# Bank reads of VectorE at the front of its queue, forget gate and keys on ScalarE, later norm sums, and another priority for h rows in a hybrid decoder layer

## The chip, the cores and the metric

The kernel runs on one core of a Trainium2 chip. The metric is the device time of one execution in microseconds (us), as the median of several runs. The engines are TensorE (PE, with its weight loads shown apart as PEld), VectorE (DVE), ScalarE (ACT), GpSimd (POOL) and SyncE (SP), which issues most of the transfers. Each has its own queue of instructions; semaphores tie them together.

## The reference

One decoder layer over 2048 tokens of width 1024, in float32. A token mixer (RMSNorm with scale and shift from a conditioning vector, one combined input projection, three groups of heads, a gated norm per head, an output projection) is followed by a channel mixer (a second norm, an up-projection, a causal convolution of width 3, a SiLU-gated product, a down-projection) and a last norm. The change touches the token mixer. For one group of heads, HGRN2, it computes:

```python
z = split_heads(hf, HG_HEADS)
lbh = lb.reshape(HG_HEADS, HG_DK)[None, :, None, :]
log_f = jnp.logaddexp(jnp.log1p(-lbh) + jax.nn.log_sigmoid(z), jnp.log(lbh))   # f = lb + (1 - lb) * sigmoid(z)
key_h = (1.0 - lbh) * jax.nn.sigmoid(-z)
o_h = gated_state_chunkwise(jax.nn.silu(split_heads(hq, HG_HEADS)), key_h, split_heads(hi, HG_HEADS), log_f)
o_h = merge_heads(rms_norm(o_h)) * jax.nn.silu(hg)
```

`gated_state_chunkwise` is a linear recurrence whose state decays by `f` for each key channel: S_t = diag(f_t) S_(t-1) + k_t^T v_t, o_t = q_t S_t. The GLA heads use the same recurrence with another gate, the retention heads one with a fixed decay. The gate of each head's output is silu(g) = g * sigmoid(g).

## The kernel before

**Blocks and units.** The token mixer goes through the sequence in four blocks of 512 tokens (`b` is 0 to 3). In each block seven units follow one another (`ORDER`): HGRN2 units h0 and h1, the GLA unit g, h2, h3, and the retention units r0 and r1. A unit projects the block's normed rows `h` with its columns of the input weights and then starts a recurrence. After the units comes the first half of the output projection (`out_half(b, 0)`). The second half (`out_finish`) runs inside the next block's unit h1. The channel mixer (from about 1250 us on) is not changed.

**Matmuls.** Each float32 operand is split into a high and a low part, and each product takes three matmuls (`split3`, L254 to L256: high by high, high by low, low by high). The casts to the high part are on ACT, the subtractions for the low part on DVE. Projections write to four PSUM banks in turn (`acc_ps`). A bank is free for a later projection once all that read it are through. Two banks serve the levels of the recurrences (`lev_ps`), two the rest (`late_ps`: norm sums and spreads, state updates, outputs, transposes).

**A unit h** (`unit_h`) projects the forget gate into one bank. ACT takes sigmoid(z) (`sf`, L742) and sigmoid(-z) (`sn`, L743) from it. DVE makes f = sf * (1 - lb) + lb (L744) and the keys kq = sn * (1 - lb) (L745). The query projection goes into the next bank: ACT takes its sigmoid (L748), DVE multiplies the bank by it (L749). Then DVE's `near` (L611 to L615) and `decays` (L626) prepare the recurrence from queries, keys and f. Values and gates of a pair of units are projected together by `tf512` into four banks, one for every 128 tokens; `tok_evac4` takes them out: a copy of the values (ACT, L559), a sigmoid of the gate (ACT, L560), and the product of the gate with its sigmoid (DVE, L561), for each bank and each of two units. `tok_evac` (L550 to L552) does this for the first two units of the first block, which project alone.

**A recurrence** (`gated`) is a chain of short steps: two transposes and their sums for neighbouring tokens (L639, L643, L649), six levels of pairwise scores, each with matmuls (`lvh` or `lvg`, L662), then DVE's multiplication of queries and keys by the level's decay (L670, L672) and a masked copy (L681 on DVE, L678 on ACT). The matmuls of a level read the queries and keys that the level before has left. Then come the keys' transpose, the states' updates (`u` at L701; L709 and L711 on DVE), the outputs (L594, L596), the norm and gate of each head (`post`, L565 to L574), and later the transpose for the output projection (L580, L583, L584). `retention` is shorter.

**Order of the work.** PE's queue is in the order in which the program issues its matmuls. A small clock written by hand (`Clock`) sets that order: every piece of projection advances it by its estimated time, and `clock.at(us, fn)` has `fn` issued when the clock has come that much further. `clock.chain(gen, us)` puts a recurrence in line: it starts `us` later at the earliest, one chain at a time, and each step names the gap until the next. `clock.until(...)` issues what is due next, whatever the clock says, until a condition holds; `out_finish` inside unit h1 is preceded by such a call, for the last transposes of the block before (L1154).

The queues of DVE, ACT and SP are filled by a planner that works at build time: it simulates the engines, and of the instructions that it thinks ready it takes the one with the smallest number, which is its place in the program. `tc.high_priority(offset=n)` lowers the numbers inside by n. `HOT` is 600, `CHAIN` 400; the recurrences' DVE and ACT work runs at `CHAIN`, the low parts of the weights (L247, L316) and the additions to the residual (L986) at `HOT`. On the chip each queue runs in the order that the planner fixed.

**Norm of the next block.** `norm1_stat(b + 1)` squares and sums the next block's rows, as small jobs between projections. After the last, `clock.at(14.0, rstd(..., gap=9.5))` puts the sum over features (`ssn`, four transposes, L337, into a `late_ps` bank) 14 us later on the clock, and 9.5 us after that the spread of the reciprocal root over the partitions (`bcn`, L348). `norm1_h(b + 1)` then loads the rows again and makes `h`: `scaled` (DVE, L365), `high` (ACT, L369), `low` (DVE, L372), one row tile after the other, while the output projection and the last chains of block b run.

Of the kernel before, what the change touches and what calls it, by code (L numbers as in the profile page):

```python
# [14 lines left out]
AF = mybir.ActivationFunctionType  # L15
ALU = mybir.AluOpType
PSUM = bass.MemoryType.PSUM

P = 128
# [30 lines left out]
HOT = 600  # L50
CHAIN = 400
# [53 lines left out]
def trunk(ctx, tc, xT, vecs, cvec, cst, rope, msk, wada, win, walow, wgla, wout, wup, wdown, out):  # L105
# [13 lines left out]
    clock = Clock()  # L119
# [13 lines left out]
    def tmp(name, shape=(P, 512)):  # L133
        return pt.tile(list(shape), F32, tag="te", name=name, bufs=NTE)
# [4 lines left out]
    def small(name, n=8):  # L139
        return pc.tile([P, n], F32, tag="sm", name=name, bufs=8)  # L140

    V, S, G, T = nc.vector, nc.scalar, nc.gpsimd, nc.tensor
# [10 lines left out]
    def newton(x, y, n):  # L153

        V.tensor_scalar(y[:].bitcast(I32), x[:].bitcast(I32), -0.5, MAGIC, op0=ALU.mult, op1=ALU.add)
        a = small("nw", n)
        for _ in range(3):
            V.scalar_tensor_tensor(a[:], y[:], -0.5, y[:], op0=ALU.mult, op1=ALU.mult)
            V.tensor_tensor(a[:], a[:], x[:], op=ALU.mult)
            V.scalar_tensor_tensor(y[:], a[:], 1.5, y[:], op0=ALU.add, op1=ALU.mult)  # L160


    oml = p1.tile([P, 4], F32, tag="oml", name="oml")
    lb = p1.tile([P, 4], F32, tag="lb", name="lb")
# [99 lines left out]
    def cf_gemm(name, i, parts=(slice(0, TB),)):  # L264
        if name in ready:
            return ready.pop(name)
        hi, lo = piece(win[i], name, f"i{i}")
        ps = acc_ps("ps" + name)
        for ts in parts:
            for k in range(KD):  # L270
                sl = slice(k * P, (k + 1) * P)
                split3(ps[:, ts], (hi[:, sl], lo[:, sl]), (h[k][:, 0, ts], h[k][:, 1, ts]), k == 0, k == KD - 1)
                adv(3 * M512)
        return ps
# [55 lines left out]
    def rstd(acc, name, bc, then, bank=None, gap=4.5):  # L330

        bank = bank or late_ps

        def first():
            p = bank("ss" + name)
            for c in range(NCH):
                T.transpose(p[:, c * P:(c + 1) * P], acc[:, c * P:(c + 1) * P], ident)  # L337
            x, r = small("ms" + name, NCH), small("rs" + name, NCH)
            with tc.high_priority(offset=CHAIN):
                V.tensor_reduce(x[:], p[:].rearrange("p (c d) -> p c d", c=NCH), axis=mybir.AxisListType.X, op=ALU.add)  # L340
                V.tensor_scalar(x[:], x[:], 1.0 / D, EPS, op0=ALU.mult, op1=ALU.add)
                newton(x, r, NCH)
            clock.at(gap, lambda: second(r))

        def second(r):
            p = bank("bc" + name)
            for c in range(NCH):
                T.transpose(p[:, c * P:(c + 1) * P], r[:, c:c + 1].to_broadcast([P, P]), ident)  # L348
            S.copy(bc, p[:])
            then()  # L350
        return first

    def sumsq(acc, x, k, name, sl=slice(0, TB), first=None):
        if k == 0 if first is None else first:
            S.activation(acc[:, sl], x[:, sl], AF.Square)
        else:
            sq = late(f"sq{name}{k}")
            S.activation(sq[:, sl], x[:, sl], AF.Square)
            V.tensor_tensor(acc[:, sl], acc[:, sl], sq[:, sl], op=ALU.add)

    def new_acc(name):
        return px.tile([P, TB], F32, tag="ssacc", name="sa" + name, bufs=1)

    def scaled(t, bc, k):
        V.scalar_tensor_tensor(t, t, SC1[:, k:k + 1], bc, op0=ALU.mult, op1=ALU.mult)  # L365

    def high(t, k, name):
        h[k] = ph.tile([P, 2, TB], F32R, tag="h", name=f"ha{name}{k}", bufs=8)
        S.activation(h[k][:, 0, :], t, AF.Identity, bias=SH1[:, k:k + 1])  # L369

    def low(t, k):
        V.scalar_tensor_tensor(h[k][:, 1, :], t, SH1[:, k:k + 1], h[k][:, 0, :], op0=ALU.add, op1=ALU.subtract)  # L372

    xs = {}
    bc1 = {}
    done = set()
# [9 lines left out]
    def new_bc1(b):  # L386
        return px.tile([P, TB], F32, tag="bc1", name=f"bc1_{b}", bufs=1)
# [111 lines left out]
    def norm1_stat(b):  # L499
        acc = []  # L500

        def load(k):
            if not acc:
                acc.append(new_acc(f"n1_{b}"))
            x = tmp(f"x{b}_{k}")
            nc.sync.dma_start(x[:], xT[b, :, k, :])
            return x

        def add(x, k):
            sumsq(acc[0], x, k, f"n1_{b}_")  # L510
            if k == KD - 1:
                bc1[b] = new_bc1(b)
                clock.at(14.0, rstd(acc[0], f"n1_{b}", bc1[b][:], lambda: done.add(("n1", b)), gap=9.5))
        for k in range(KD):
            jobs.append((0.7, lambda k=k: load(k), lambda x, k=k: add(x, k)))

    def norm1_h(b):
        clock.until(lambda: ("n1", b) in done)
        for k in range(KD):
            t = tmp(f"xn{b}_{k}")  # L520
            nc.sync.dma_start(t[:], xT[b, :, k, :])
            scaled(t[:], bc1[b][:], k)
            high(t[:], k, f"{b}_")
            low(t[:], k)


    def new_qbd(name, rows):

        q = p1.tile([P, 2, TB], F32, tag="qbd", name="qb" + name, bufs=3)
        for hh in range(2):  # L530
            G.memset(q[64 * hh:64 * hh + 64, 1 - hh, :], 0.0)
            if rows[hh][1] - rows[hh][0] < 64:
                G.memset(q[64 * hh:64 * hh + 64, hh, :], 0.0)
        return q
# [5 lines left out]
    def tok_tiles(name):  # L540

        return (pu.tile([P, NCH, P], F32, tag="v", name="v" + name, bufs=4),
                pu.tile([P, NCH, P], F32, tag="sg", name="sg" + name, bufs=4))

    def tok_evac(vsg, pss):
        v, sg = vsg
        for j, ps in enumerate(pss):
            p3 = ps[:].rearrange("p (c n) -> p c n", n=256)
            c2 = slice(2 * j, 2 * j + 2)
            S.copy(v[:, c2, :], p3[:, :, 0:P])  # L550
            S.activation(sg[:, c2, :], p3[:, :, P:256], AF.Sigmoid)
            V.tensor_tensor(sg[:, c2, :], sg[:, c2, :], p3[:, :, P:256], op=ALU.mult)  # L552

    def tok_evac4(vsg, pss, at):

        v, sg = vsg
        for c, ps in enumerate(pss):
            gate = ps[:, at + P:at + 256]
            S.copy(v[:, c, :], ps[:, at:at + P])  # L559
            S.activation(sg[:, c, :], gate, AF.Sigmoid)  # L560
            V.tensor_tensor(sg[:, c, :], sg[:, c, :], gate, op=ALU.mult)  # L561

    def post(o, sg, name):

# [170 lines left out]
    def unit_h(b, u, pos, between=None):  # L735
        nm = f"h{b}_{u}"
        kq = pu.tile([P, TB], F32, tag="k", name="k" + nm, bufs=3)
        f = pu.tile([P, TB], F32, tag="f", name="f" + nm, bufs=3)
        e = pu.tile([P, TB], F32, tag="e", name="e" + nm)
        ps = cf_gemm("hf" + nm, 4 * u + 1)  # L740
        sf, sn = tmp("sf" + nm), tmp("sn" + nm)
        S.activation(sf[:], ps[:], AF.Sigmoid)  # L742
        S.activation(sn[:], ps[:], AF.Sigmoid, scale=-1.0)  # L743
        V.tensor_scalar(f[:], sf[:], oml[:, u:u + 1], lb[:, u:u + 1], op0=ALU.mult, op1=ALU.add)  # L744
        V.tensor_scalar(kq[:], sn[:], oml[:, u:u + 1], None, op0=ALU.mult)  # L745
        ps = cf_gemm("hq" + nm, 4 * u)
        sq = tmp("sq" + nm)
        S.activation(sq[:], ps[:], AF.Sigmoid)  # L748
        V.tensor_tensor(sq[:], ps[:], sq[:], op=ALU.mult)  # L749
        xy = near(sq, kq, f, nm)  # L750
        rows = [(0, 64), (64, 128)]
        q = new_qbd(nm, rows)
        for hh, (r0, r1) in enumerate(rows):
            V.tensor_tensor(q[r0:r1, hh, :], sq[r0:r1, :], f[r0:r1, :], op=ALU.mult)
        decay = decays(f, e)
        subs = [(q, rows, *tok_tiles(nm))]
        clock.chain(gated(nm, b, u, pos, kq, decay, subs, xy), 9.0 if b == u == 0 else 6.0)
        if b == 0 and u < 2:
            tok_evac(subs[0][2:], tf_gemm("vg" + nm, 4 * u + 2))
            tokens.add(nm)  # L760
            return
        waiting[nm] = subs[0][2:]
        if between:
            between()
        if u % 2:
            pss = tf512("vg" + nm, 4 * u - 2, 4)
            for i, one in enumerate((f"h{b}_{u - 1}", nm)):
                tok_evac4(waiting.pop(one), pss, 256 * i)
                tokens.add(one)
# [364 lines left out]
    for b in range(NB):  # L1134
        pos = 0
# [511 lines left out]
```

## Time and profile before

| | us |
|---|---|
| median of 3 runs | 2535.63 |
| lowest and highest run | 2533.63, 2539.6 |
| the profiled execution | 2533.2 |
| its span on the core | 2531.4 |
| token mixer, all blocks | about 60 to 1250 |
| channel mixer | about 1250 to 2531 |

The profile shows one execution, taken on the core by the hardware. Times are microseconds from the start of the span. A line with an engine, a kernel line and a tile name stands for a group of instructions; "<-" in a name leads from what is written to what is read. A row of waits names who waited for whom, the time in total, the number of waits and the longest. A row of stretches gives, after the stretch and its length, the busy time and number of instructions of PE, PEld, DVE, ACT and POOL, then PE's granted clock as a share of full speed, the share of the transfer engines, and GB/s. In a row of the timeline stand start, duration, engine, line, operation, tiles, and in brackets the idle time before it with what ended it. In a row of groups stand, after the count, the busy time, the mean in ns, and the idle time of the engine just before, with what ended it.

### The profile page before, as it was taken

To read this page: it belongs to the slowest core of one execution; us is meant where nothing else is said; L and a number is where in the kernel's file an instruction comes from. 1 tells how busy PE (TensorE), PEld (TensorE's weight loads), DVE (VectorE), ACT (ScalarE), POOL (GpSimd) and SP (SyncE) were. 2 spreads that over 40 slices of the span, in tenths; PEclk is the share of its full clock that TensorE was granted. 3 is DMA by queue.
4 is the path that set the end of the run, shared out by engine and by line. 5 is a ranking of instruction groups with operands and counts; after the bars stand their busy time and mean duration, and the time that the engine had idled before them with its cause. 6 is when DMAs were issued, how large, how long until landed. Compare 5 with 4: busy or idle time off the path is not lost.

```text
span 2531.4 us, 35178 instructions
## 1 busy us (share of the span) xinstructions
PE 2452.0 (97%) x12165; PEld 2059.3 (81%) x12165; DVE 1989.5 (79%) x3652; ACT 1147.5 (45%) x1950; POOL 146.3 (6%) x278
## 2 busy tenths in 40 slices
PE   5999999999999999999999999999989999999998
PEld 4888877888888888788788888888868888888887
DVE  8987887877688685877798888887678777778666
ACT  3334434434443434434554454455445545545442
POOL 1000000000000000000100000000001010010000
PEclk9999999999999999999999999999999999999999
DMA  8844458865689647884654544587665544447663
GB/s 312 296 159 134 169 169 322 290 234 169 215 283 318 224 157 241 311 300 158 222 190 147 171 147 141 168 283 243 209 199 186 159 137 152 150 133 263 213 196 126
DMA packets 232498, 525.11 MB, mean 207 GB/s; under 512 B 24928, under 2 KB 28032, under 8 KB 232320
## 3 DMA queue, kind: packets, MB, share of 16 engines
q1 hardware_dynamic: 229120, 512.38, 60.0%
q0 software_dynamic: 3200, 10.49, 1.2%
q8 instruction: 96, 1.57, 0.2%
q14 instruction: 82, 0.67, 0.1%
HBM read 397.46 MB, written 125.30 MB: 207 GB/s over the span
## 4 chain that ended last, share of the span: by engine, by line
PE 82%; DVE 8%; DMA 5%; issue 2%; ACT 1%; SPq 0%; DVEq 0%; POOL 0%; ACTq 0%; POOLq 0%
PE X L254 6%; PE X L256 6%; PE X L255 6%; PE Z L256 3%; PE Z L255 3%; PE Z L254 3%; PE lvh L662 3%; PE dX L256 3%; PE dX L255 3%; PE dX L254 3%; PE psqkvgr L254 2%; PE psqkvgr L256 2%; PE psqkvgr L255 2%; PE y L254 2%; PE y L256 2%
## 5 line engine op out<-in xcount | busy, mean ns | idle before, releaser
L254 PE MATMUL X<-B,A 128*128 128x512 f32 x572 | 224.4, 392 | 1.4 <-ACT u L1354 1.4
L255 PE MATMUL X<-B,A 128*128 128x512 f32 x572 | 223.9, 391 | 0.0
L256 PE MATMUL X<-B,A 128*128 128x512 f32 x572 | 223.6, 391 | 0.0
L1055 DVE TENSOR_TENSOR dA<-rd,dA 128x512 fp32r<-128x512 f32 x154 | 106.0, 689 | 87.6 <-ACT dA L1054 87.5
L1054 ACT CAST dA<-rd 128x512 fp32r<-128x512 f32 x154 | 95.6, 621 | 138.8 <-PE dY L256 42.2
L1055 DVE TENSOR_TENSOR A<-s,A 128x512 fp32r<-128x512 f32 x176 | 120.7, 686 | 40.7 <-ACT A L1054 40.3
L1054 ACT CAST A<-s 128x512 fp32r<-128x512 f32 x176 | 108.6, 618 | 68.0 <-PE Z L256 45.2
L254 PE MATMUL dX<-dB,dA 128*128 128x512 f32 x352 | 136.9, 389 | 0.0
L255 PE MATMUL dX<-dB,dA 128*128 128x512 f32 x352 | 136.9, 389 | 0.0
L256 PE MATMUL dX<-dB,dA 128*128 128x512 f32 x352 | 136.9, 389 | 0.0
L254 PEld LDWEIGHTS X<-B,A 128*128 128x128 f32 x572 | 108.2, 189 | 24.5 <-ACT u L1354 2.2
L255 PEld LDWEIGHTS X<-B,A 128*128 128x128 f32 x572 | 108.2, 189 | 22.7
L256 PEld LDWEIGHTS X<-B,A 128*128 128x128 f32 x572 | 108.2, 189 | 22.7
L255 PE MATMUL Z<-B,A 128*128 128x512 f32 x308 | 120.0, 390 | 2.2 <-DVE B L1055 2.2
L254 PE MATMUL Z<-B,A 128*128 128x512 f32 x308 | 119.9, 389 | 0.0
L256 PE MATMUL Z<-B,A 128*128 128x512 f32 x308 | 119.8, 389 | 0.0
L662 PEld LDWEIGHTS lvh<-qbh,kh 128*128 128x128 f32 x768 | 100.5, 192 | 17.0 <-issue 9.2
L1055 DVE TENSOR_TENSOR dB<-rb,dB 128x512 fp32r<-128x512 f32 x154 | 105.6, 686 | 10.2 <-ACT dB L1054 10.1
L1055 DVE TENSOR_TENSOR A<-r,A 128x512 fp32r<-128x512 f32 x130 | 89.3, 687 | 29.4 <-ACT A L1054 29.1
L662 PE MATMUL lvh<-qbh,kh 128*128 128x128 f32 x768 | 102.8, 277 | 7.3 <-DVE kh L672 7.1
L1054 ACT CAST A<-r 128x512 fp32r<-128x512 f32 x130 | 81.0, 623 | 62.4 <-PE Z L256 60.0
L254 PE MATMUL psqkvgr<-hqkvgr,ha 128*128 128x512 f32 x256 | 106.1, 415 | 1.1 <-DVE orsg L160 1.0
(475 smaller groups left out, 6981.2 us busy)
## 6 DMA issues: line engine op xcount, KB each, us to landing
gs<-yv SPq DMA_DIRECT2D x154, 256.0 KB, 2.9
rb<-gs SPq DMA_DIRECT2D x154, 256.0 KB, 3.9
r<-wup SPq DMA_DIRECT2D x140, 256.0 KB, 3.3
s<-sumsu SPq DMA_DIRECT2D x136, 256.0 KB, 3.0
wada<-wada SPq DMA_DIRECT2D x48, 512.0 KB, 6.0
rd<-sumsd SPq DMA_DIRECT2D x88, 256.0 KB, 3.8
rd<-wdown SPq DMA_DIRECT2D x66, 256.0 KB, 3.9
x<-xT SPq DMA_DIRECT2D x64, 256.0 KB, 5.8
```

The lines of the kernel that those rows point to most:

```text
L254: T.matmul(ps, lhs[0], rhs[0], start=first, stop=False, skip_group_check=more)
L255: T.matmul(ps, lhs[0], rhs[1], start=False, stop=False, skip_group_check=more)
L256: T.matmul(ps, lhs[1], rhs[0], start=False, stop=last, skip_group_check=more)
L662: T.matmul(ps[:, c * P:(c + 1) * P].rearrange("p (h n s) -> p h n s", h=2, s=s), kq[:, c * P:(c + 1) * P], rhs, start=True, stop=True)
L1054: S.copy(hi, src)
L1055: V.tensor_tensor(lo, src, hi, op=ALU.subtract)
```

## The change

Six edits, all in the token mixer:

1. The products of a gate or query bank with its sigmoid (L552, L561, L749 of the kernel before) get the offset `HOT`.
2. The forget gate f and the keys kq are made by ACT, with a scale (and for f a bias) for each partition, in place of DVE.
3. The rows of `norm1_h` (`scaled`, `high`, `low`) get the offset `CHAIN`.
4. The norm sum of `norm1_stat` is due 20 us after the last square, in place of 14.
5. The spread follows it after 14 us, in place of 9.5.
6. The chain of block 1's first unit h0 starts 9 us after its projections, in place of 6, as block 0's does.

```diff
-                clock.at(14.0, rstd(acc[0], f"n1_{b}", bc1[b][:], lambda: done.add(("n1", b)), gap=9.5))
+                clock.at(20.0, rstd(acc[0], f"n1_{b}", bc1[b][:], lambda: done.add(("n1", b)), gap=14.0))
...
-            scaled(t[:], bc1[b][:], k)
-            high(t[:], k, f"{b}_")
-            low(t[:], k)
+            with tc.high_priority(offset=CHAIN):
+                scaled(t[:], bc1[b][:], k)
+                high(t[:], k, f"{b}_")
+                low(t[:], k)
...
-            V.tensor_tensor(sg[:, c2, :], sg[:, c2, :], p3[:, :, P:256], op=ALU.mult)
+            with tc.high_priority(offset=HOT):
+                V.tensor_tensor(sg[:, c2, :], sg[:, c2, :], p3[:, :, P:256], op=ALU.mult)
...
-            V.tensor_tensor(sg[:, c, :], sg[:, c, :], gate, op=ALU.mult)
+            with tc.high_priority(offset=HOT):
+                V.tensor_tensor(sg[:, c, :], sg[:, c, :], gate, op=ALU.mult)
...
-        V.tensor_scalar(f[:], sf[:], oml[:, u:u + 1], lb[:, u:u + 1], op0=ALU.mult, op1=ALU.add)
-        V.tensor_scalar(kq[:], sn[:], oml[:, u:u + 1], None, op0=ALU.mult)
+        S.activation(f[:], sf[:], AF.Identity, scale=oml[:, u:u + 1], bias=lb[:, u:u + 1])
+        S.activation(kq[:], sn[:], AF.Copy, scale=oml[:, u:u + 1])
         ps = cf_gemm("hq" + nm, 4 * u)
         sq = tmp("sq" + nm)
         S.activation(sq[:], ps[:], AF.Sigmoid)
-        V.tensor_tensor(sq[:], ps[:], sq[:], op=ALU.mult)
+        with tc.high_priority(offset=HOT):
+            V.tensor_tensor(sq[:], ps[:], sq[:], op=ALU.mult)
...
-        clock.chain(gated(nm, b, u, pos, kq, decay, subs, xy), 9.0 if b == u == 0 else 6.0)
+        clock.chain(gated(nm, b, u, pos, kq, decay, subs, xy), 9.0 if u == 0 and b < 2 else 6.0)
```

## The prediction

> **What bounds the kernel now.** I read the first part of the page, then stretches of busy time, then what the matmul queue waited for.
>
> ```profile
> span 2531.4 us, 35178 instructions
> PE 2452.0 (97%) x12165; PEld 2059.3 (81%) x12165; DVE 1989.5 (79%) x3652; ACT 1147.5 (45%) x1950; POOL 146.3 (6%) x278
> ```
>
> The profiled execution took 2533.2 us, 1.8 around its span; the median of the runs is 2535.63, 2.4 above it. TensorE (PE) sets the time: only its idle time and its slow time can be won.
>
> ```profile
> 60.00:1250.00 1190.00, 1162.52 (x6411) 993.36 (x6409) 945.76 (x2177) 485.70 (x923) 49.47 (x98) 0.99 0.67 231
> 262.00:310.00 48.00, 46.11 (x253) 39.54 (x253) 45.05 (x101) 20.78 (x43) 2.08 (x4) 0.99 0.52 179
> ```
>
> The change touches the token mixer, about 60 to 1250 us. There PE is idle 1190 - 1162.5 = 27.5 us. VectorE (DVE) is busy 79% of the stretch, but 94% (45.05 of 48) where one block gives way to the next: PE's waits there are waits for DVE's queue. The view of waits names them:
>
> ```profile
> PE lvh L662 <- DVE kh L672: 7.1, 6, 3.8
> PE pshfh L254 <- DVE sgg L561: 4.5, 1, 4.5
> PE psvgh L254 <- DVE sqh L749: 3.7, 1, 3.7
> PE ssn L337 <- DVE S L711: 2.6, 1, 2.6
> PE pshfh L255 <- DVE ha L372: 1.9, 1, 1.9
> PE psqkvgr L254 <- DVE orsg L160: 1.0, 1, 1.0
> PE alg L790 <- DVE sgh L561: 0.6, 1, 0.6
> ```
>
> A long wait costs more than itself. These are the stretches just after five of them; the third number from the right is the granted clock:
>
> ```profile
> 177.00:184.00 7.00, 6.90 (x26) 6.19 (x27) 5.29 (x11) 1.04 (x1) 0.00 (x0) 0.57 0.13 48
> 309.00:316.00 7.00, 7.00 (x44) 6.56 (x45) 1.67 (x4) 3.17 (x6) 0.00 (x0) 0.76 0.45 150
> 343.00:350.00 7.00, 6.53 (x32) 6.02 (x33) 6.01 (x13) 0.69 (x1) 0.00 (x0) 0.76 0.42 129
> 792.00:799.00 7.00, 6.95 (x45) 6.32 (x46) 6.75 (x24) 1.94 (x3) 1.04 (x2) 1.00 0.60 203
> 1045.00:1052.00 7.00, 6.45 (x20) 5.18 (x21) 3.02 (x9) 0.08 (x1) 0.00 (x0) 0.65 0.80 281
> ```
>
> After the waits of 3.7 (product sq), 1.9 (h rows), 3.8 (level) and 4.5 us (product sg) PE runs part of 7 us slowly: 7 x (1 - clock) is 3.0, 1.7, 1.7 and 2.5 us lost. After the 2.6 us wait at 792 nothing is.
>
> **The change part by part.** *1. The query product (L749) to the front.* It frees the bank that the next projection waits for.
>
> ```profile
> 170.88 0.60 ACT L748 ACTIVATE sqh<-pshqh 128x512 f32<-128x512 f32 x1
> 176.36 0.69 DVE L749 TENSOR_TENSOR sqh<-pshqh,sqh 128x512 f32<-128x512 f32 x1
> 177.10 0.80 PE L254 MATMUL psvgh<-hvgh,ha 128*128 128x512 f32 x1 [3.66 <-DVE sqh L749]
> ```
>
> Its sigmoid was done at 171.48, but the product began at 176.36, behind level work and sums. PE needed the bank at 177.10 - 3.66 = 173.44. In front of the queue the product could follow the sigmoid; the two operations that ScalarE (ACT) now gets may push the sigmoid back by 1.4 us (part 3), so the product ends near 171.5 + 1.4 + 0.7 = 173.6. Gain 3.66 + 3.0 less 0.2: 6.4; bounds 3 and 6.7.
>
> *2. The gate products (L561, L552) to the front.*
>
> ```profile
> 1038.10 0.28 ACT L560 ACTIVATE sgg<-psvgg 128x128 f32<-128x128 f32 x1
> 1041.30 0.28 ACT L560 ACTIVATE sgg<-psvgg 128x128 f32<-128x128 f32 x1
> 1041.46 1.05 ACT L242 CAST hhfh<-rhfh 128x1024 fp32r<-128x1024 f32 x1
> 1042.95 0.29 DVE L561 TENSOR_TENSOR sgg<-sgg,psvgg 128x128 f32<-128x128 f32 x1
> ```
>
> Three of four banks had their first sigmoid by 1038.4, and DVE took the first product at 1042.95. PE stood from 1041.1. What is late next is ACT: the second half of the first bank still needs copy, sigmoid and product, some 0.3 us each. If it goes ahead of the last bank nothing is left of the wait; behind that bank's sigmoid (to 1041.6) some 0.9 us is, behind the cast 2. I take 1.1: 4.45 + 2.45 - 1.1 = 5.8; bounds 3 and 6.9.
>
> *3. Forget gate and keys to ACT.*
>
> ```profile
> L744 DVE TENSOR_SCALAR fh<-sfh,oml,lb 128x512 f32<-128x512 f32 x15 | 8.1, 542 | 3.1 <-ACT sfh L742 3.0
> L745 DVE TENSOR_SCALAR kh<-snh,oml 128x512 f32<-128x512 f32 x15 | 7.2, 482 | 0.0
> L369 ACT ACTIVATE ha<-xn,mod 128x512 fp32r<-128x512 f32 x24 | 16.9, 720 | 33.6 <-DVE xn L365 33.5
> ```
>
> DVE loses 8.1 + 7.2 = 15.3 us. ACT gains 2 x 15 operations; the nearest row, with an operand per partition, is 0.72 us: 21.6 us, on an engine busy 486 of 1190. Both run during the next projection, which hides them: their reader needs the query product too. Without that cover it would be 1.4 us a unit. By itself nothing; the 15 us pay for part 7.
>
> *4. h rows at the recurrences' priority.*
>
> ```profile
> 305.68 0.72 ACT L369 ACTIVATE ha<-xn,mod 128x512 fp32r<-128x512 f32 x1 [2.98 <-DVE xn L365]
> 308.16 0.75 DVE L372 SCALAR_TENSOR_TENSOR ha<-xn,mod,ha 128x512 fp32r<-128x512 f32 x1
> ```
>
> The last low part could have started at 306.4 and did at 308.16, behind chain work that the rows now precede. It would end near 307.1, where PE began to wait. Gain 1.89 + 1.7 less 0.2: 3.4. With DVE full here the displaced work could be late in its turn: bounds 0 and 3.6.
>
> *5. The chain of block 1's first unit starts 3 us later.*
>
> ```profile
> 340.56 1.22 DVE L247 TENSOR_TENSOR lwo<-rwo,hwo 128x1024 fp32r<-128x1024 f32 x1
> 342.90 0.42 DVE L672 TENSOR_TENSOR kh<-kh,eh 128x256 f32<-128x256 f32 x1
> 343.47 0.55 PE L662 MATMUL lvh<-qbh,kh 128*128 128x128 f32 x1 [3.77 <-DVE kh L672]
> ```
>
> Here the kernel runs all due work up to the last transpose of the block before, so two levels stand back to back in PE's queue, and the second needs DVE's work on the first. Started 3 us later, one level fewer is due by then, and the level ahead of it is issued some 2 us earlier; a wait near 1.7 is left. Gain 2.1, and half of the 1.7 of slow clock: 3.0; bounds 0 and 5.5.
>
> [...]
>
> *6. Room for norm sums and spreads.*
>
> ```profile
> 200.82 0.60 PE L348 MATMUL bcn<-c_all,rsn 128*128 128x128 f32 x4
> L365 DVE SCALAR_TENSOR_TENSOR xn<-xn,mod,bc x24: 743/745/753, 280.3 to 904.8; 128x512 f32<-128x512 f32 x24
> ```
>
> The sum that waited 2.64 us for the state updates to leave its bank comes 6 us later: gain 2.6, bounds 0 and 2.6. The spread comes 10.5 us later in all, at about 211 in place of 200.8 in the first block; its first reader ran at 280.3, so this costs nothing there. No spread of the mixer waited, so the wider gap wins nothing.
>
> *7. What the front of the queue costs.*
>
> ```profile
> L749 DVE TENSOR_TENSOR sqh<-pshqh,sqh 128x512 f32<-128x512 f32 x16 | 11.0, 685 | 9.7 <-ACT sqh L748 9.7
> L561 DVE TENSOR_TENSOR sgh<-sgh,psvgh 128x128 f32<-128x128 f32 x56 | 15.6, 285 | 10.2 <-ACT sgh L560 9.7
> L561 DVE TENSOR_TENSOR sgr<-sgr,psqkvgr 128x128 f32<-128x128 f32 x32 | 9.0, 285 | 25.6 <-ACT sgr L560 25.5
> L561 DVE TENSOR_TENSOR sgg<-sgg,psvgg 128x128 f32<-128x128 f32 x32 | 8.2, 281 | 0.4 <-ACT sgg L560 0.3
> L372 DVE SCALAR_TENSOR_TENSOR ha<-xn,mod,ha 128x512 fp32r<-128x512 f32 x24 | 17.7, 745 | 0.2
> L365 DVE SCALAR_TENSOR_TENSOR xn<-xn,mod,bc 128x512 f32<-128x512 f32 x24 | 17.6, 746 | 0.3 <-DMA xn<-xT 0.3
> L670 DVE TENSOR_TENSOR qbh<-qbh,eh 128x512 f32<-128x512 f32 x80 | 55.0, 688 | 27.0 <-PE lvh L662 25.9
> ```
>
> 11.0 + 32.8 + 35.3 = 79 us of DVE work moves ahead of the recurrences' chain, whose levels PE waits for, against 15 us that leave DVE. The last row shows DVE ahead of PE for 25.9 us at these levels, so there is slack in many of them, not in all. Bounds 0 and the 32.8 of the gate products, were all of it on the path. The nearest row is the present wait of levels, 7.1; I let as much again come: 7. The short waits of 1.0 and 0.6, both near bank reads, I count as 1.0 won (bounds -2 and 3).
>
> Sum: 6.4 + 5.8 + 3.4 + 3.0 + 2.6 + 1.0 - 7 = 15.2 us won. That is 2518.0 for the profiled execution and 2520.4 on the median. The sums of the bounds: 28.3 won without part 7, and 6 - 2 - 32.8 = 28.8 lost.
>
> **Rivals.** *Slower: DVE stands at the front.* A product put first holds all behind it until its sigmoid is there. Already now DVE idles 9.7 + 9.7 + 25.5 + 0.3 = 45 us in front of such products, in some 35 waits, so 1.3 us each. There are 45 places (15 units, and 120 products in groups of four). In half of them, 23 x 1.3 = 30 us of the chain's slack gone, and in 5 a slow clock of 1.7, makes 38; less the 22 won it is 16 lost: 2551. It decides from 17 places on (22 / 1.3). For it: DVE's 94% at the block's end. Against it: the idle time that DVE has at the levels. Chance 0.12. [...]
>
> *The same: the waits move.* DVE's work before PE's waits is nearly the same, and other readers wait as long: the 27.5 us of idle time stay, 2531 to 2540. Chance 0.2.
>
> *The priority does little.* Queue places follow the planner's own forecast of when an operand is ready; where that is off, the products stay where they were. Then parts 5 and 6 alone work, 5.6 won: 2530. Chance 0.08.
>
> *All waits go and none comes:* 28 won, 2507. Chance 0.1.
>
> **How the numbers follow.** The forecast has 0.5, at 2520, its own range 2512 to 2529. With 0.12 left out above and half of the last rival below, the range is 2508 to 2538. A measurement of this kernel can tell about 0.2%, 5 us, from no change. Faster: 0.5 + 0.1 + half of 0.08, 0.64. The same: 0.2 and 0.02 of the third rival, 0.22. Slower: 0.12 and the last 0.02 of the third, 0.14.
>
> **What would show it.** Right: no wait of PE for L749 or L561 over 1 us, granted clock 1.00 where it was 0.57 and 0.65; no wait of the norm sum for L711; PE idle in the mixer near 15 us. Wrong: longer waits of lvh or lvg for L672, of the o matmuls for L711 or L709, more idle time of DVE before L561, or ACT's sigmoid L748 more than 1.5 us later behind the new operations.

## The result, and the profile after

The changed kernel takes 2551.6 us (median of 6 runs, 2547.1 to 2559.9) against 2535.0 for the kernel before: a ratio of 1.0065, with a 95% interval of 1.0053 to 1.0076. It is 17 us slower; the forecast was 15 us faster. The profiled execution is the shortest of the six, 2547.05, with a span of 2545.3, which is 13.9 more than before. Line numbers are those of each kernel; in the changed one they stand 3 or 4 higher (L711 became L714, L749 became L753, L561 became L564).

The first part of the page, after:

```profile
span 2545.3 us, 35173 instructions
PE 2456.5 (97%) x12165; PEld 2063.4 (81%) x12165; DVE 1978.6 (78%) x3620; ACT 1167.7 (46%) x1982; POOL 145.6 (6%) x278
```

DVE lost 11 us of work and ACT gained 20; worked out were 15 and 22. PE still sets the time. The view of PE's waits, after, only the token mixer's largest:

```profile
PE lvh L665 <- DVE kh L675: 8.4, 8, 2.2
PE oh L597 <- DVE S L714: 7.5, 3, 3.0
...
PE or L599 <- DVE atr L907: 4.9, 2, 2.4
...
PE ug L704 <- ACT kTg L693: 2.4, 1, 2.4
...
PE oTh L583 <- DVE oh L577: 1.6, 2, 1.0
PE og L597 <- DVE S L714: 1.6, 1, 1.6
```

The targets are gone from this list: no wait for the query product, none of the gate products over 0.2 us, none of the norm sum for the state updates, none for the h rows. The longest wait of a level fell from 3.8 to 2.2 us, though the levels wait a little more in all. In their place stand waits of the output matmuls for the recurrences' state updates (L714) and for retention's masked scores (L907), which before had 0.2 us between them.

They lie at the changes of block. I took the stretch from the start of the last product of unit r1's projection to the start of the next block's query projection, which holds the same work in both kernels. Before, for blocks 0 to 1, 1 to 2 and 2 to 3:

```profile
267.86:309.74 41.88, 39.99 (x220) 34.19 (x219) 39.33 (x86) 17.55 (x30) 2.08 (x4) 0.99 0.53 180
576.90:622.32 45.42, 45.42 (x266) 39.81 (x265) 42.31 (x111) 20.97 (x34) 4.06 (x8) 1.00 0.49 166
871.37:917.03 45.66, 45.51 (x265) 39.64 (x264) 42.04 (x111) 20.50 (x35) 4.06 (x8) 1.00 0.48 165
```

After:

```profile
264.79:310.31 45.52, 41.62 (x220) 35.24 (x220) 40.23 (x86) 17.47 (x30) 2.08 (x4) 0.96 0.51 166
574.84:630.62 55.78, 50.59 (x264) 44.60 (x263) 44.02 (x112) 20.66 (x34) 4.06 (x8) 0.91 0.39 135
880.39:934.92 54.53, 49.07 (x265) 43.15 (x264) 43.95 (x112) 20.62 (x35) 4.07 (x8) 0.94 0.41 138
```

The three take 3.6, 10.4 and 8.9 us longer, 22.9 in all. That is more than the whole span's 13.9, so the rest of the kernel is 9.0 us faster. Within the 22.9, PE's idle time (length less busy time) went from 2.0 to 14.6, 12.5 more. The slow clock, length times one less the granted clock, went from 0.4 to 10.1, 9.7 more. Taken together, the added idle time is paid nearly twice.

DVE's queue at the change from block 1 to 2 shows where its first long wait comes from. The timeline of DVE, before:

```profile
584.07 0.75 DVE L372 SCALAR_TENSOR_TENSOR ha<-xn,mod,ha 128x512 fp32r<-128x512 f32 x1
584.74 0.27 DVE L711 SCALAR_TENSOR_TENSOR S<-S,eh,uh 64x64 f32<-64x64 f32 x1
584.93 0.74 DVE L986 SCALAR_TENSOR_TENSOR x<-y,mod,x 128x512 f32<-128x512 f32 x1
585.68 2.16 DVE L711 SCALAR_TENSOR_TENSOR S<-S,eh,uh 64x64 f32<-64x64 f32 x7
```

After, with the matmul that waits (from the timeline of PE) behind it:

```profile
581.18 0.57 DVE L714 SCALAR_TENSOR_TENSOR S<-S,eh,uh 64x64 f32<-64x64 f32 x2
582.12 1.50 DVE L365 SCALAR_TENSOR_TENSOR xn<-xn,mod,bc 128x512 f32<-128x512 f32 x2 [0.37 <-DMA xn<-xT]
583.66 0.75 DVE L990 SCALAR_TENSOR_TENSOR x<-y,mod,x 128x512 f32<-128x512 f32 x1
584.61 0.75 DVE L365 SCALAR_TENSOR_TENSOR xn<-xn,mod,bc 128x512 f32<-128x512 f32 x1 [0.20 <-DMA xn<-xT]
585.28 2.07 DVE L372 SCALAR_TENSOR_TENSOR ha<-xn,mod,ha 128x512 fp32r<-128x512 f32 x3
587.27 0.89 DVE L714 SCALAR_TENSOR_TENSOR S<-S,eh,uh 64x64 f32<-64x64 f32 x3
```

```profile
587.91 0.58 PE L597 MATMUL oh<-S,qbh 128*128 128x128 f32 x1 [2.75 <-DVE S L714]
```

The eight updates of the state ran as one and seven, about 3 us; now six operations of the h rows stand between the second and the third, and the third starts 5.5 us after the second has ended: about 4.3 us of it are the rows' operations, 0.7 an addition to the residual that stood among the updates before too, 0.6 DVE's standing for the rows' transfers. The matmul that reads it stands 2.75 us, and PE starts no other from 585.16 to 587.91.

### The profile page after: what moved, and what is told of

It is laid out like the page before. It is cut to its first block, busy times and chain, and to the rows that moved or that the text cites. A ratio compares the mean times of both kernels' runs of the same rounds, so it can differ in the third digit from the quotient of the medians.

```text
span 2545.3 us, 35173 instructions
## 1 busy us (share of the span) xinstructions
PE 2456.5 (97%) x12165; PEld 2063.4 (81%) x12165; DVE 1978.6 (78%) x3620; ACT 1167.7 (46%) x1982; POOL 145.6 (6%) x278
## 4 chain that ended last, share of the span: by engine, by line
PE 76%; DVE 9%; DMA 9%; ACT 2%; issue 2%; SPq 0%; DVEq 0%; ACTq 0%
PE X L254 6%; PE X L255 6%; PE X L256 6%; PE Z L255 3%; PE Z L256 3%; PE Z L254 3%; PE dX L255 3%; PE dX L254 3%; PE dX L256 3%; PE lvh L665 2%; PE psqkvgr L254 2%; PE psqkvgr L256 2%; PE psqkvgr L255 2%; PE dY L255 2%; PE dY L254 2%
```

## The experiments

The theory that the profile suggests (A): edit 3, the h rows at `CHAIN`, costs more than 20 us, because the rows pass the recurrences' steps in DVE's queue. The rival from the prediction (B): the bank products at the front make DVE stand. The first expectation counts under A also that DVE stands idle until the rows' transfers and ScalarE's part are there; from the run with the rows at offset 100 on, this standing is a rival of its own, E.

**The changed kernel with edit 3 undone.**

```diff
-            with tc.high_priority(offset=CHAIN):
-                scaled(t[:], bc1[b][:], k)
-                high(t[:], k, f"{b}_")
-                low(t[:], k)
+            scaled(t[:], bc1[b][:], k)
+            high(t[:], k, f"{b}_")
+            low(t[:], k)
```

> The changed kernel with the h rows at their old place (edit 3 undone, all else kept). Theory A: the rows, put ahead of the state updates and the masked scores, hold VectorE while they wait for transfers and ScalarE, and cost some 20 us at the three changes of block (waits of the o matmuls for L714 of 1.8, 2.7, 3.0 us and for L907 of 2.4 us twice, and the slow clock after them). Then this run is at 2525 to 2532, under the kernel before, and PE's waits for L714 and L907 at the changes of block are gone. Rival B: the products at the front of the queue cost it (VectorE standing before L564 and L753); then undoing the rows alone leaves 2545 to 2552.

Measured: 2527.6 us, ratio 0.9972 (0.9961 to 0.9983). The change of block 1 to 2 is back at its length, with the full clock:

```profile
574.17:619.83 45.66, 45.51 (x265) 39.64 (x264) 42.05 (x111) 20.54 (x34) 4.07 (x8) 1.00 0.49 165
```

Edit 3 is the loss and rival B falls: one edit of six turns a gain of 0.3% into a loss of 0.65%. By which way the rows cost it, this run does not tell.

**Edit 3 alone**, on the kernel before.

```diff
-            scaled(t[:], bc1[b][:], k)
-            high(t[:], k, f"{b}_")
-            low(t[:], k)
+            with tc.high_priority(offset=CHAIN):
+                scaled(t[:], bc1[b][:], k)
+                high(t[:], k, f"{b}_")
+                low(t[:], k)
```

> The kernel before with the h rows at CHAIN (edit 3 alone). Theory A: 2550 to 2558, since the 17 us lost in all and whatever the other edits won add up; waits of the o matmuls for state updates and of or for atr at the changes of block 1 to 2 and 2 to 3, some 10 us each with the slow clock. Rival B: within 5 us of 2535.

Measured: 2555.6 us, 1.0088 (1.0071 to 1.0104): 22 us by the ratio, 20 by the medians (2535.7 before). Its waits of PE, the rows that were not there before:

```profile
PE oh L595 <- DVE S L712: 8.8, 4, 3.4
...
PE or L597 <- DVE atr L904: 3.7, 2, 2.5
```

The three changes of block, taken as above, sum to 155.1 us against 133.0 before: 22.2 more, the whole loss (the span is 22.4 longer). The edit costs about the same alone and among the others, 22.2 and 22.9 there.

At the change of block 1 to 2 this run also tells the passing of the chain from the standing for transfers. DVE's timeline, and the matmul that waits:

```profile
587.31 0.57 DVE L712 SCALAR_TENSOR_TENSOR S<-S,eh,uh 64x64 f32<-64x64 f32 x2
587.90 0.75 DVE L365 SCALAR_TENSOR_TENSOR xn<-xn,mod,bc 128x512 f32<-128x512 f32 x1
588.57 0.75 DVE L372 SCALAR_TENSOR_TENSOR ha<-xn,mod,ha 128x512 fp32r<-128x512 f32 x1
589.25 0.75 DVE L365 SCALAR_TENSOR_TENSOR xn<-xn,mod,bc 128x512 f32<-128x512 f32 x1
589.92 0.75 DVE L372 SCALAR_TENSOR_TENSOR ha<-xn,mod,ha 128x512 fp32r<-128x512 f32 x1
590.70 0.27 DVE L712 SCALAR_TENSOR_TENSOR S<-S,eh,uh 64x64 f32<-64x64 f32 x1
```

```profile
592.01 0.79 PE L595 MATMUL oh<-S,qbh 128*128 128x128 f32 x2 [3.20 <-DVE S L712]
```

Between the second and the third update DVE does not stand at all: four operations of the rows fill the gap, a fifth follows the third update, and PE waits 3.2 us behind them. Ahead of the first update DVE had stood 0.6 us for a transfer.

**Edit 1 alone**: the bank products at `HOT`, on the kernel before; likewise for the other gate product and the query product.

```diff
-            V.tensor_tensor(sg[:, c, :], sg[:, c, :], gate, op=ALU.mult)
+            with tc.high_priority(offset=HOT):
+                V.tensor_tensor(sg[:, c, :], sg[:, c, :], gate, op=ALU.mult)
```

> The kernel before with the bank products at HOT (edit 1 alone). Theory A: the waits for L749 at 173 and L561 at 1041 go with their slow clock, some 12 us won less what the chain loses: 2522 to 2531. Rival B: 2545 to 2555, with more idle time of VectorE before L561 than the 35 us of before and longer waits of the levels.

Measured: 2528.6 us, 0.9973 (0.9959 to 0.9986), 7 us won. PE waits neither for the query product nor for the gate product of block 3; where the clock had been 0.57, it is full (7 us from 177):

```profile
177.00:184.00 7.00, 7.00 (x40) 6.02 (x40) 6.97 (x16) 0.77 (x2) 0.00 (x0) 1.00 0.46 152
```

Two other waits have come in the mixer, of the norm's spread (L348) for a head's norm, 2.7 us, and of a state matmul for ACT, 2.5 in place of 0.7; they are part of why 7 us are won and not the 12 of both targets. Rival B's sign is missing too. DVE stands before the gate products as long as before (10.6 + 25.1 + 0.3 us against 10.2 + 25.6 + 0.4), and before the query products 10.4 against 9.7.

**Edit 2 alone**: forget gate and keys on ACT, on the kernel before.

```diff
-        V.tensor_scalar(f[:], sf[:], oml[:, u:u + 1], lb[:, u:u + 1], op0=ALU.mult, op1=ALU.add)
-        V.tensor_scalar(kq[:], sn[:], oml[:, u:u + 1], None, op0=ALU.mult)
+        S.activation(f[:], sf[:], AF.Identity, scale=oml[:, u:u + 1], bias=lb[:, u:u + 1])
+        S.activation(kq[:], sn[:], AF.Copy, scale=oml[:, u:u + 1])
```

> The kernel before with forget gate and keys on ScalarE (edit 2 alone). Theory A: nothing by itself, 2530 to 2538: VectorE loses 15 us, ScalarE gains 21, neither on PE's path. A rival C: ScalarE's sigmoid L748 comes later behind the two new operations and PE's wait for the query product grows: 2540 to 2545.

Measured: 2534.1 us, 0.9995 (0.9983 to 1.0008): nothing that can be told. DVE stands 14.1 us before the query products in place of 9.7, for their sigmoid, which ACT now takes after the two new operations; PE's wait for them is 2.0 and did not grow.

**The edits of the clock alone** (4, 5 and 6), on the kernel before.

```diff
-                clock.at(14.0, rstd(acc[0], f"n1_{b}", bc1[b][:], lambda: done.add(("n1", b)), gap=9.5))
+                clock.at(20.0, rstd(acc[0], f"n1_{b}", bc1[b][:], lambda: done.add(("n1", b)), gap=14.0))
...
-        clock.chain(gated(nm, b, u, pos, kq, decay, subs, xy), 9.0 if b == u == 0 else 6.0)
+        clock.chain(gated(nm, b, u, pos, kq, decay, subs, xy), 9.0 if u == 0 and b < 2 else 6.0)
```

> The kernel before with the edits of the clock alone (4, 5 and 6: norm sums and spreads later, block 1's first chain later). Theory A: the waits of 2.6 us (ssn for L711) and most of 3.8 us (lvh at 340) go with a slow clock of 1.7: 3 to 6 us won, 2529 to 2533. Rival D: other waits take their place as they did for the rows: 2534 to 2538.

Measured: 2538.0 us, 1.0012 (1.0003 to 1.0021), a small loss, at the upper end of rival D's range. The norm sum no longer waits for the states, and the levels wait 2.9 us in all, against 7.1. But a new row stands high in PE's waits:

```profile
PE psqkvgr L254 <- ACT sgh L560: 5.4, 2, 3.6
```

The longer of the two waits ends at 518.3. In DVE's timeline just before it, the norm sum's work (L340, and its Newton steps at L158) now runs into the gate products of h2 and h3 (L561), which have no priority in this kernel, while the next projection wants their banks:

```profile
513.33 0.69 DVE L340 TENSOR_REDUCE msn<-ssn 128x4 f32<-128x512 f32 x1
514.00 0.28 DVE L561 TENSOR_TENSOR sgh<-sgh,psvgh 128x128 f32<-128x128 f32 x1
...
516.79 0.28 DVE L561 TENSOR_TENSOR sgh<-sgh,psvgh 128x128 f32<-128x128 f32 x1
```

ACT's later copies and sigmoids of the same banks come only after these products: it stood 2.8 us until its copy at 514.32 and 0.7 until that at 517.11, both for L561. PE's matmul at 518.26 comes after ACT's sigmoid at 517.96. A level's work and another head's norm stand in the same stretch, so the share of the norm sum in this wait is not shown.

**The rows at offset 100** in place of 400, all other edits kept.

```diff
-            with tc.high_priority(offset=CHAIN):
+            with tc.high_priority(offset=100):
```

> The changed kernel with the rows at offset 100 in place of CHAIN (400): still ahead of work without an offset, but behind the state updates, which VectorE's queue now has in one run ahead of the rows. Theory A (it is the passing of the chain that costs): as with the rows put back, 2524 to 2531, no wait of the o matmuls for state updates over 1 us. Rival E: any earlier place of the rows costs, since VectorE then stands for their transfers: 2538 to 2552, with idle time of VectorE before L365 as large as with CHAIN (5.5 us when the edit stood alone).

Measured: 2521.9 us, 0.9952 (0.994 to 0.9964), the lowest median of all runs and 2 us under theory A's range. Its trace, that of its fastest execution, has all eight state updates ahead of the rows in DVE's queue:

```profile
575.88 1.84 DVE L714 SCALAR_TENSOR_TENSOR S<-S,eh,uh 64x64 f32<-64x64 f32 x6
...
578.42 0.58 DVE L714 SCALAR_TENSOR_TENSOR S<-S,eh,uh 64x64 f32<-64x64 f32 x2
579.04 2.08 DVE L365 SCALAR_TENSOR_TENSOR xn<-xn,mod,bc 128x512 f32<-128x512 f32 x3
```

DVE stands 0.4 us for the rows' transfers, and the change of block is as short as before:

```profile
569.54:614.87 45.33, 45.33 (x265) 39.72 (x263) 41.92 (x111) 20.64 (x34) 4.06 (x8) 1.00 0.50 166
```

So an earlier place for the rows is no loss in itself, and rival E falls in this form. Since the standing went together with the passing of the chain, this run alone does not part the two. One wait for a state update over 1 us is left against the expectation, 1.3 in unit g at 787, away from the changes of block.

**State updates and masked scores ahead of the rows**, which stay at `CHAIN`. Three blocks of the chain go from `CHAIN` to `2 * HOT`: the updates in `gated` and in `retention`, and the masking of the scores in `retention`.

```diff
-            with tc.high_priority(offset=CHAIN):
+            with tc.high_priority(offset=2 * HOT):
                 for c in range(nk):
                     for hh, (r0, r1) in enumerate(rows):
...
-        with tc.high_priority(offset=CHAIN):
+        with tc.high_priority(offset=2 * HOT):
             for c in range(nk):
                 dst = Sst[:, (b * NCH + c + 1) % NS, :]
...
-            with tc.high_priority(offset=CHAIN):
+            with tc.high_priority(offset=2 * HOT):
                 V.tensor_tensor(at[:, j * 512:(j + 1) * 512].rearrange("p (a n) -> p a n", n=P),
```

> The changed kernel, rows at CHAIN as they are, but the state updates (L714, L895) and the masked scores (L907) at an offset of 1200, so that these two pass the rows. Theory A: the waits for L714 (7.5 us) and L907 (4.9 us) go with their slow clock of some 6 us; the rest of the chain (norms, kkr) is still late: 2533 to 2542. Rival E: VectorE standing before the rows is the cost, so 2546 to 2553 as the changed kernel.

Measured: 2549.1 us, 1.0064 (1.005 to 1.0078), a miss of theory A's number. The trace is that of its slowest execution, 2556. The waits for the masked scores went and those for state updates fell to 0.9 us, as it said. But these rows came:

```profile
PE oTh L583 <- DVE nw L158: 8.9, 2, 4.5
...
PE kTr L873 <- DVE nw L158: 6.0, 2, 3.3
```

kTr transposes retention's decayed keys (L860), oTh the normed outputs (`post`): the chain's next steps, still behind the rows. DVE's timeline at the change of block 1 to 2, where PE's transposes stood until 605.4, shows the keys behind the last rows:

```profile
603.15 0.74 DVE L372 SCALAR_TENSOR_TENSOR ha<-xn,mod,ha 128x512 fp32r<-128x512 f32 x1
603.81 0.17 DVE L573 TENSOR_SCALAR omsh<-omsh 128x8 f32<-128x8 f32 x1
603.88 0.69 DVE L916 TENSOR_TENSOR or<-or,c_all 128x512 f32<-128x512 f32 x1
604.49 0.16 DVE L155 TENSOR_SCALAR orsh<-omsh 128x8 int32<-128x8 int32 x1
604.55 0.69 DVE L860 TENSOR_TENSOR kkr<-ra1r,c_all 128x512 f32<-128x512 f32 x1
```

The other new wait, 4.5 us of oTh until 612.6, has a second source, which is this run's own edit. Retention's updates, now at the largest offset, hold the last steps of a head's norm (L158 to L160) back:

```profile
606.89 0.16 DVE L158 SCALAR_TENSOR_TENSOR nw<-orsh 128x8 f32<-128x8 f32 x1
608.22 2.45 DVE L895 SCALAR_TENSOR_TENSOR S<-S,c_all,ur 64x64 f32<-64x64 f32 x8 [1.17 <-PE ur L883]
610.68 0.17 DVE L159 TENSOR_TENSOR nw<-nw,omsh 128x8 f32<-128x8 f32 x1
```

DVE stands 1.2 us in front of them until PE has their sums, and works 2.45 on them; in the changed kernel they alternate with the norm's steps. The same comes again at 916 to 919. So the run is no clean test of the number: it took two steps out of the rows' way and put the end of a norm behind one of them. The number fits rival E, the trace does not: DVE stood 2.7 us for the rows' transfers here, less than the 3.4 of the changed kernel. What it does show is that the masked scores and updates are not the only steps that the rows make late; the keys are too.

**The low parts alone at `CHAIN`**, the scaling and the high parts at their old place.

```diff
             scaled(t[:], bc1[b][:], k)
             high(t[:], k, f"{b}_")
-            low(t[:], k)
+            with tc.high_priority(offset=CHAIN):
+                low(t[:], k)
```

> The changed kernel with only the low part of the rows (L372) at CHAIN, the scaling and the high part at their old place. Theory A: the low parts become ready one at a time, behind work that keeps its old order, so that they pass little of the chain: 2524 to 2534, and the wait of 1.9 us for L372 at 307 may go. Rival E: a third to a half of the rows' loss: 2535 to 2545.

Measured: 2523.1 us, 0.9963 (0.9949 to 0.9978), 1 us under theory A's range, and the wait of the projections for the rows at 307 is gone. The reason given beforehand, that the low parts depend on a scaling which stayed behind the chain and so can pass little of it, fits this but was not tested by itself.

**The rows' loads at `CHAIN` too.**

```diff
-            nc.sync.dma_start(t[:], xT[b, :, k, :])
             with tc.high_priority(offset=CHAIN):
+                nc.sync.dma_start(t[:], xT[b, :, k, :])
                 scaled(t[:], bc1[b][:], k)
```

> The changed kernel with the rows' loads at CHAIN too, so that VectorE waits less for transfers at the front of its queue. Its queue has the same order at the changes of block: two state updates, six operations of the rows, six state updates. Theory A (the chain passed by the rows is the cost): 2546 to 2554, the waits for L714 and L907 stay. Rival E (standing for transfers is the cost): idle time before L365 from some 5 us to under 2 and the time down by twice that or more, 2538 to 2545.

Measured: 2549.6 us, 1.005 (1.0037 to 1.0064). As a test of rival E it is inconclusive, since the loads did not come sooner: DVE stood 5.5 us before L365, not less than the changed kernel's 3.4. What bounds that rival is this: in the changed kernel all of DVE's standing before rows is 3.4 us for transfers and 2.0 for ACT, against the 12.5 us by which PE's idle time grew. So standing can make up less than half of that idle time, even if PE waited for every microsecond of it, and at most 0.6 of the 3.2 us wait shown for edit 3 alone; its exact share stays open.

**The rows at offset 100 alone**, on the kernel before.

```diff
-            scaled(t[:], bc1[b][:], k)
-            high(t[:], k, f"{b}_")
-            low(t[:], k)
+            with tc.high_priority(offset=100):
+                scaled(t[:], bc1[b][:], k)
+                high(t[:], k, f"{b}_")
+                low(t[:], k)
```

> The kernel before with the rows at offset 100 alone. Against the changed kernel the offset won 5 to 6 us more than putting the rows back (2521.9 and 2527.6). If that belongs to the rows' place, this run is at 2528 to 2532 beside 2535; if it is chance of the order, or hangs on the products at the front, 2533 to 2538.

Measured: 2537.0 us, 1.0002 (0.9993 to 1.0011): nothing. The 5.7 us by which offset 100 beat the rows put back do not belong to the rows alone; the intervals of those two runs touch (0.9964 and 0.9961), so they may be noise in part.

**Products, ACT and rows at 100, without the clock's edits**; against the version with the rows at 100:

```diff
-                clock.at(20.0, rstd(acc[0], f"n1_{b}", bc1[b][:], lambda: done.add(("n1", b)), gap=14.0))
+                clock.at(14.0, rstd(acc[0], f"n1_{b}", bc1[b][:], lambda: done.add(("n1", b)), gap=9.5))
...
-        clock.chain(gated(nm, b, u, pos, kq, decay, subs, xy), 9.0 if u == 0 and b < 2 else 6.0)
+        clock.chain(gated(nm, b, u, pos, kq, decay, subs, xy), 9.0 if b == u == 0 else 6.0)
```

> The kernel before with the products at HOT, forget gate and keys on ScalarE, and the rows at offset 100, without the three edits of the clock. Alone these lost 3 us, by a collision of the later norm sum with gate products that had no priority; with the products at the front that collision should be gone. If the clock's edits then win something, this run is above the 2521.9 with them, 2524 to 2530; if not, 2518 to 2523.

Measured: 2532.3 us, 0.9983 (0.9973 to 0.9992), above the range for "they win something". With the clock's edits the same kernel is at 0.9952, and the intervals lie apart: those edits lose 0.12% alone and win 0.31% beside edits 1 and 2 and the rows at 100. The traces tell where. Without the clock's edits the norm's spread (L348) waits 3.8 us at 512 and the norm sum 2.6 at 791; with them, 0.5 and none. The spread waits like this also with edit 1 alone (2.7), but not in the kernel before, with edit 2 alone or with the rows at 100 alone: by these traces it is the products at the front that make the wider gap worth having.

**The best version without edit 2**; against the version with the rows at 100:

```diff
-        S.activation(f[:], sf[:], AF.Identity, scale=oml[:, u:u + 1], bias=lb[:, u:u + 1])
-        S.activation(kq[:], sn[:], AF.Copy, scale=oml[:, u:u + 1])
+        V.tensor_scalar(f[:], sf[:], oml[:, u:u + 1], lb[:, u:u + 1], op0=ALU.mult, op1=ALU.add)
+        V.tensor_scalar(kq[:], sn[:], oml[:, u:u + 1], None, op0=ALU.mult)
```

> The best version so far (2521.9: products at HOT, gate and keys on ScalarE, the clock's edits, rows at 100), with forget gate and keys back on VectorE. Theory: alone the move to ScalarE won nothing that can be told (0.9995), so 2519 to 2525. Rival F: VectorE needs the 15 us where the products now go first; then 2526 to 2533, with longer waits of the levels for L672's work.

Measured: 2525.1 us, 0.9964 (0.9947 to 0.9981), at the upper end of the theory's range. Its interval overlaps that of the best version, so what ACT's share is worth there stays open.

## Why the prediction was wrong

**The step that failed is part 4, and part 7 with it.** Part 4 gave the rows' new priority a gain of 3.4 us with bounds 0 and 3.6; it measured 22 us lost, alone and within the change. It looked at the one place where the rows were late, and let the displaced chain work cost at most the gain itself. Part 7 did count the rows' 35.3 us among the 79 that move ahead. But it took its upper bound from the gate products alone, and its value of 7 from the waits of levels. The levels have slack (before, DVE stood 25.9 us in all until PE's level matmuls were through); the state updates and masked scores that the rows passed at the changes of block have little, since DVE is 93% busy there (42.3 of 45.4 us) and PE reads them soon: before, at block 1 to 2, the pairs of updates that the outputs read ended at 585.97, 586.60 and 587.22 and were each read 1.2 to 1.3 us later, the first masked scores ended at 598.20 and were read 2.3 us later. The row for that was to be had before: in the stretch of 45.42 us PE had no idle time at all, so nothing was there to take up a delay beyond that slack. After, the stretch is 10.4 us longer, with 5.2 us of idle time and 5.0 of slow clock. What share of the loss is DVE's standing for the rows, and not its work on them, stays open, below the bound given above.

**Parts 1 and 2** held. Both waits and their slow clock are gone in the changed kernel (granted clock 1.00 from 177 to 184 and from 1056 to 1063). Alone the products won 7 us, where these parts with the whole charge of part 7 make 12.2 - 7 = 5.2. Part 7 looked for that charge in the levels; the trace of edit 1 alone has the levels at 5.6 in place of 7.1 and the new waits at the norm's spread and a state matmul.

**Part 3** held: 0.9995 alone. On ACT the keys take the 0.72 us taken for each of the two operations, the forget gate, with its scale and bias, 0.82:

```profile
L747 ACT ACTIVATE fh<-sfh,lb,oml 128x512 f32<-128x512 f32 x16 | 13.0, 816 | 0.1
L748 ACT ACTIVATE kh<-snh,oml 128x512 f32<-128x512 f32 x16 | 11.5, 719 | 0.0
```

**Parts 5 and 6** were mis-sized for want of an interaction. They were to win 5.6; alone they lost 3, beside the other edits they win some 8 (0.9983 to 0.9952). The norm sum was taken as four transposes with a bank to wait for; its DVE work, a reduction and Newton steps at `CHAIN`, moves with it and, in the run of these edits alone, stands among the gate products. And part 6 gave the wider gap nothing, since no spread waited before; with the products at the front one waits 3.8 us, and the gap takes that away. Of the level's wait of 3.8 that part 5 aimed at, two waits of 1.0 and 2.2 are left in the changed kernel, more than the 1.7 forecast, but with the clock full.

**The rivals.** The slower rival named 2551 and the time came out there by luck, since the mechanism is another. DVE stands before the gate products about as long as it did (8.7 + 24.3 + 0.5 us against 10.2 + 25.6 + 0.4). Before the query products it stands 15.9 us in place of 9.7; edit 1 alone had 10.4 and edit 2 alone 14.1, so most of the increase is the sigmoid that ACT takes later, and alone it cost nothing. The text's own list named the right sign, longer waits of the o matmuls for L711, without giving it a rival, a price or a chance.

**The granted clock.** The length of a single wait does not tell in these traces whether a slow clock follows it. Before, 0.76 followed a wait of 1.9 us and 1.00 one of 2.6. Around the waits of 2.75 and 2.44 us that end at 588 and 606, the clock of the changed kernel is 0.91 over 56 us, with 0.50 from 590 to 593 and 0.53 from 608 to 611. Around its wait of 2.2 us that ends at 342.8 it is full, though another of 1.0 ended at 339:

```profile
340.00:347.00 7.00, 4.38 (x25) 3.34 (x24) 6.89 (x13) 0.69 (x1) 0.00 (x0) 1.00 0.48 152
```

## What to carry to other kernels

A priority moves an operation past everything between its old place and its new one. List what it passes, and ask of each passed step how soon the bounding engine reads it; where that engine has no idle time in the stretch, nothing takes up the delay, and here 5.2 us of new idle time came with 5.0 of slow clock. Lift work just above what may wait, not up to what may not: the same rows at 100 cost nothing alone and belong to the best version, at 400 they lost 0.9%. A raised step that still waits for its operands can hold back what is ready behind it: put first, retention's state updates kept DVE standing 1.2 us and working 2.45, and a norm step whose operand was done at 607.05 ran at 610.68. And edits that are worth nothing or lose alone can win together, so take an edit out of the whole as well as trying it alone.

## What the runs showed of the hardware

At the three changes of block of the changed kernel, with waits of 1.7 to 3.0 us, slow clock cost TensorE nearly as much as the waits did: 12.5 us more idle time came with 9.7 us more of slow clock. Around another wait of that kind, of 2.2 us at 340, the clock was full (1.00 over 7 us); what decides between them was not tried. Within the changed kernel's runs, the recorded granted clock over the whole span went from 0.992 in the two of 2547 us to 0.986 in that of 2560.
